# Ten side chains of a hybrid decoder step issued later or on VectorE, and a residual added over two down groups

## The chip, the cores and the metric

The kernel runs on one core of a Trainium2 chip, as one launch. The time is the device time of that core in microseconds (us). The engines are named as in the profile: PE (matmul), PEld (weight load), DVE (VectorE), ACT (ScalarE), POOL (GpSimd) and SP (SyncE, which issues most DMAs).

## The reference

One decoder layer for 1024 prompt positions and 64 sample positions (8 sequences of 8 new tokens), which share the weights:

```python
x = x + 0.5 * swiglu(rmsnorm(x), ffn1_w_gu, ffn1_w_down)        # FFN1, D_MODEL 1024, D_FF 2816
h = rmsnorm(x); z = h @ w_in
y_att = attend(q, k, v, rel_bias)      # 3 head groups (window, dilation) (128,1) (512,4) (2048,16), combined by softmax denominators
xc = causal_conv(xr); hr = rglru(xc)   # recurrent branch, 768 wide
y_rec = gelu(yr) * hr
y_mem = memory_attention(qm, mk, mv)   # 4 heads, 256 memory tokens
merged = sum_b sigmoid(gate_b) * (y_b @ W_b_o);  x = x + merged @ w_out
x = x + 0.5 * swiglu(rmsnorm(x), ffn2_w_gu, ffn2_w_down)        # FFN2
y = rmsnorm(x, final_norm)
```

The sample positions attend to cached keys and values of up to 2048 positions, as well as to each other.

## The kernel before

All data is float32. Every large product is made of three matmuls on split operands (`mac3`, lines 262, 263 and 264: high times high, high times low, low times high), so each weight tile has to be split first: ACT copies the high part (L167), DVE subtracts it for the low part (L168).

The order on PE, ACT, DVE and POOL is that in which the Python code issues the instructions. Only SP's order is left to the scheduler. Each engine takes its instructions in order, so an instruction that waits holds up all that stand behind it.

**Ticks.** `mac3` calls `tick()` in the middle of a long product, and the tile routines call it at the end of one. A tick runs what `later(n, f)` has put n ticks ahead, then, every second tick, one step (up to the next `yield`) of each of the first two generators in `K.side`; odd ticks serve `K.first`. So a further `yield` means that the rest of a side chain is issued two ticks later, behind more matmuls. `drain(*K.side)` at the end of a stage calls `tick()` with no product between, until the side chains are through.

**FFN start** (`operands_of_blocks`, `norms_of_blocks`, `gain_blocks`, `sums_of_blocks`): squares on ACT (L411) are added up on DVE (L413), then `rstd` reduces them with small matmuls (L294) and `put_rows` spreads the result with transposes (L306, L307). Meanwhile PE runs the first `plain` products; their results stay in PSUM banks (`held`) until the row is known, and `evacuate(n)` says how many may stay. `sums_of_blocks` subtracts blocks (L437) that the later operands `put(tp, 6)` and `put(tp, 7)` need.

**FFN middle**: the `quad` loop forms gate and up products, `swiglu` evacuates them on DVE (L539, L554, L561), and `gated_hidden` issues silu, product and store 4, 5 and 7 ticks later (1, 3 and 4 for the last `ALONE` units). `first_hidden` loads back the first four hidden tiles and splits them (`hidden`, L573 on ACT, L574 on DVE). `down` then goes over groups of hidden rows, and each result tile is added to x (L648). In FFN2 `residual(o)` loads a row of the old x (`xr`) and adds it on POOL eight ticks later (L1822); it is called for all eight rows of x in group 1.

**FFN1 end**: for each row tile, `sumsq` squares on ACT and adds on POOL (L321), or on DVE into `odd`; `norm_chunk` then makes the row as above.

**Attention and sample chain**: the heads loop runs on PE with `heads_prep` at the side. `sample_job` is another side chain. For each of three groups, `sample_scores` goes over 16 steps: fetch a key piece and a broadcast query `qb` (DMA from `qs_d`, SP), multiply on POOL (L978, 128x1024), and one step later sum on DVE (L968). Then, for each group and half q, `sample_values` makes the softmax (L1004 to L1012), pads the transposed weights (L1020 to L1025), multiplies by the cached values (L1041, L1043, added up by L1047 or L1049) and selects the heads (L1051, L1053). At the end `sample_mix` combines the groups and transposes (L1068).

**LRU stage**: six `lru_tile`s, each with two z tiles of `w_in` and some gate tiles, a convolution on DVE (L1312 to L1321), gate products (L1332), scan on DVE (L1360) and gelu. `att_combine` is a side chain there: it transposes finished rows (L835), and `mix_groups` weights and adds up the three groups (L858 to L876). The rest of `sample_job` runs at the side too. PSUM banks with the tag "t" are two, shared by L835, the sample chain and others. The stage ends with

```python
            while K.due:
                K.tick()
            drain(*K.side)
```

In the order that the code issues, `sample_job` ends at tick 928 and the last product of the stage is at tick 930. The merge follows.

Of the kernel before, what the change touches and what calls it, by code (L numbers as in the profile page):

```python
# [12 lines left out]
OP = mybir.AluOpType  # L13
# [9 lines left out]
KF = DFF // 128  # L23
# [22 lines left out]
PLAIN, ALONE = 3, 2  # L46
# [14 lines left out]
class Kernel:  # L61
# [329 lines left out]
    def norms_of_blocks(self, tp, xs, pool, eng):  # L391

        nc = self.nc

        def rstd(j, acc):
            r = self.rstd(TC, acc)
            t0 = tp * TH + j * TC

            def put_rows():
                self.rows(self.rbc[:, t0:t0 + TC], r, TC)  # L400
                self.known.add((tp, j))
            self.later(3, put_rows)
        for j in range(2):
            acc = pool.tile([128, TC], F32, name=self.uid("acc"), tag="mu", bufs=2)
            for i in range(2):
                for k in range(4):
                    if i or k:
                        t = self.sums.tile([128, 512], F32, name=self.uid("sq"), tag="s2", bufs=2)[:, :TC]
                    else:
                        t = acc  # L410
                    nc.scalar.activation(t, self.block(xs, i, j)[:, k], AF.Square)  # L411
                    if i or k:
                        eng.tensor_tensor(out=acc, in0=acc, in1=t, op=OP.add)  # L413
                if i:
                    self.later(3, lambda j=j, acc=acc: rstd(j, acc))
                yield

    def gain_blocks(self, xs, g, eng):
# [13 lines left out]
    def sums_of_blocks(self, tp, xs, eng, rest=lambda: True):  # L432

        b11, b12, b21, b22 = (self.block(xs, i, j) for i in range(2) for j in range(2))

        def less(out, x, y):
            eng.tensor_tensor(out=out, in0=x, in1=y, op=OP.subtract)  # L437
        less(b11, b12, b11)
        less(b12, b22, b12)
        less(b22, b22, b11)  # L440
        yield
        yield
        self.put(tp, 6, b22)
        yield
        self.put(tp, 7, b12)
        less(b21, b21, b22)
        yield
        while not rest():
            yield
        self.put(tp, 5, b11)  # L450
        yield
        self.put(tp, 4, b21)
        yield

    def plain(self, gu, p, order, pool):

        nc = self.nc
        ws = [self.unit(gu, 128) for _ in range(2)]
        for tp in order:
            xo = self.xo[tp]  # L460
            sl, uu = (pool.tile([128, 2, TC], F32, name=self.uid(x), tag=x, bufs=n) for x, n in (("sl", 3), ("uu", 3)))
            for j, ms in enumerate(((1, 2), (0, 3))):
                rb = self.rbc[:, tp * TH + j * TC:tp * TH + (j + 1) * TC]
                both = []
                self.evacuate(1)
                for w in ws:
                    while not all(m in xo for m in ms):
                        self.tick()
                    ps = self.mm_bank("pg")
                    self.mac3(ps[:, :TC], [(w(k, 0), (xo[ms[k // 4]][:, 0, k % 4, :], xo[ms[k // 4]][:, 1, k % 4, :]))  # L470
                                           for k in range(KD)])
                    both.append(ps)

                def evac(j=j, rb=rb, both=both, sl=sl, uu=uu, tp=tp):
                    for t, ps in zip((sl, uu), both):
                        nc.vector.tensor_tensor(out=t[:, j], in0=ps[:, :TC], in1=rb, op=OP.mult)
                    if j:
                        self.gated_hidden(p, tp, sl, uu, (2, 3, 4))
                self.held.append(((tp, j), evac))
                self.evacuate(2)  # L480
                if self.first:
                    self.tick()
        for _ in ws:
            self.done()
# [44 lines left out]
    def swiglu(self, p, tp, pool):  # L529

        nc = self.nc
        rb = self.rbc[:, tp * TH:(tp + 1) * TH].rearrange("p (j n) -> p j n", j=2)
        t = {}

        def new(name, shape, bufs):
            t[name] = pool.tile([128, *shape], F32, name=self.uid(name), tag=name, bufs=bufs)

        def plus(out, ps, x):
            nc.vector.tensor_tensor(out=out, in0=ps, in1=x, op=OP.add)  # L539

        def step(m, ps):
            if m == 1:
                new("mu", [TC], 2)
                nc.scalar.activation(t["mu"], ps, AF.Copy)
            if m == 6:
                plus(t["mu"], ps, t["mu"])
            if m == 7:
                new("uu", [2, TC], 3)
                plus(t["uu"][:, 1], ps, t["mu"])
            if m == 5:  # L550
                plus(t["uu"][:, 1], ps, t["uu"][:, 1])
            if m == 2:
                new("sl", [2, TC], 3)
                nc.vector.tensor_tensor(out=t["sl"][:, 0], in0=ps, in1=rb[:, 0], op=OP.mult)  # L554
            if m == 4:
                plus(t["uu"][:, 0], ps, t["mu"])
                nc.gpsimd.tensor_tensor(out=t["uu"], in0=t["uu"], in1=rb, op=OP.mult)
            if m == 3:
                sl = t["sl"]
                plus(sl[:, 1], ps, t["mu"])  # L560
                (nc.gpsimd if p < KF - ALONE else nc.vector).tensor_tensor(out=sl[:, 1], in0=sl[:, 1], in1=rb[:, 1], op=OP.mult)  # L561
                self.gated_hidden(p, tp, sl, t["uu"], (4, 5, 7) if p < KF - ALONE else (1, 3, 4))
        return step

    def hidden(self, k, pool, raws, wait):
# [15 lines left out]
    def first_hidden(self, pool, raws, rest):  # L581

        self.h = {}
        for k in range(2):
            self.hidden(k, pool, raws, 4 + 2 * k)
        for k in range(2, 4):
            self.later(3 + 2 * k, lambda k=k: self.hidden(k, pool, raws, 4))
        self.later(2, rest)

    def gate_up(self, gu, first, pool, copies, misc, change):  # L590
# [23 lines left out]
    def down(self, dn, pool, raws, after, residual=None):  # L614

        for g, (k, nk, w) in enumerate(DOWN):
            ks = range(k, k + nk)
            if 0 < g < len(DOWN) - 1:
                for j in range(2):
                    self.hidden(DOWN[g + 1][0] + j, pool, raws, 8 + 4 * j)  # L620
            if w == D:
                units = [self.unit(dn, w) for _ in ks]
                for c in range(3):
                    for o in range(KD):
                        self.down_tile([u(0, o * 128) for u in units], ks, o, c)
                        after(c, o)
                for _ in ks:
                    self.done()
                continue
            for o0 in range(0, KD, w // 128):  # L630
                wd = self.unit(dn, w)
                for o in range(o0, o0 + w // 128):
                    for c in range(3):
                        self.down_tile([wd(j, (o - o0) * 128) for j in range(nk)], ks, o, c, residual and g == 0)
                    if residual and g == 1:
                        residual(o)
                self.done()

# [213 lines left out]
    def mix_groups(self, o, A, H):  # L852

        nc = self.nc
        m = lambda g: o[:, g, :, H * 64:H * 64 + H]
        l = lambda g: o[:, g, :, H * 65:H * 65 + H]
        w = self.small.tile([128, 5, A, H], F32, name=self.uid("mw"), tag="mw", bufs=2)
# [6 lines left out]
        for g in range(3):  # L864
            t = w[:, 3] if g == 0 else w[:, 4]
# [5 lines left out]
            nc.vector.tensor_tensor(out=w[:, g], in0=w[:, g], in1=w[:, 4], op=OP.mult)  # L871
        oa = [o[:, g, :, 0:H * 64].rearrange("p a (h e) -> p a h e", h=H) for g in range(3)]
        for g in range(3):
            nc.gpsimd.tensor_tensor(out=oa[g], in0=oa[g], in1=w[:, g, :, :, None].to_broadcast([128, A, H, 64]), op=OP.mult)
            if g:
                nc.gpsimd.tensor_tensor(out=oa[0], in0=oa[0], in1=oa[g], op=OP.add)  # L876


    def sample_open(self, pool):
# [67 lines left out]
    def sample_scores(self, g):  # L947

        nc, p = self.nc, self.sp
# [18 lines left out]
            nc.vector.tensor_reduce(st[:, b, :, u * 4:(u + 1) * 4].rearrange("p h t -> p t h"),  # L968
                                    qb.rearrange("p t (h e) -> p t h e", h=4), axis=AX.X, op=OP.add)
        cur = fetch(0)  # L970
        yield
        prev = None
        for n in range(16):
            if n:
# [9 lines left out]
    def sample_values(self, st, g, v_new, qz, k_new):  # L984
# [17 lines left out]
        for q in range(2):  # L1002
# [11 lines left out]
            pad = p.tile([128, 4, 8, 32], F32, name=self.uid("pad"), tag="qb", bufs=2)  # L1014
            if g:
                nc.gpsimd.memset(pad[:, :, :ncl, :], 0.0)
            yield
            yield
            pp = self.bank("t")
# [277 lines left out]
    def lru_tile(self, i):  # L1297
# [5 lines left out]
        fin = p.tile([128, 36], F32, name=self.uid("fin"), tag="fin", bufs=1)  # L1303
        smp = lambda ap: ap[:, SEQ + 3:SEQ + 91].rearrange("p (b u) -> p b u", u=11)
        samp = lambda ap: ap.rearrange("p (b t) -> p b t", b=8)
        nc.gpsimd.memset(xe[:, 0:3], 0.0)
        nc.gpsimd.tensor_copy(smp(xe)[:, :, 0:3], samp(self.stT[:, i, 0:24]))

        def conv(c, ps):
            t0, n = CH[c]  # L1310
# [254 lines left out]
def emit(K):  # L1565
# [98 lines left out]
    with ExitStack() as es:  # L1664
# [6 lines left out]
        def part(c, o):  # L1671
# [3 lines left out]
                K.new_xg(c)  # L1675
                acc[c] = K.tmps.tile([128, CMAX], F32, name=K.uid("acc"), tag="acc", bufs=2)[:, :n]
            K.split_x(c, o, xa, K.v["mix_norm"])
            if c == 2 and o % 2:
                K.sumsq(o // 2, xa, odd, n, nc.vector)
            else:  # L1680
                K.sumsq(o, xa, acc[c], n)
            if o % 4 == 3:
                nc.sync.dma_start(K.x_d[0][:, o - 3:o + 1, t0:t0 + n], K.x[:, o - 3:o + 1, t0:t0 + n])
            if o == KD - 1:
                K.later(6 if c < 2 else 2, lambda: K.norm_chunk(c, 5 if c < 2 else 2, acc[c], *([odd] if c == 2 else [])))
        K.down("w_dn1", pool, K.raw_tiles(pool), after)
        K.tick()
    low.close()
# [270 lines left out]
```

## Time and profile before

| | |
|---|---|
| time, median of 3 runs | 2748.76 us (2747.99 to 2752.01) |
| the profiled execution | 2746.11 us |
| its span | 2744.3 us |
| mean granted TensorE clock | 0.989 |

The profile is of one execution. The busy share of PE is that of matmuls with modelled ends. "Idle before, releaser" in a row is the time for which the engine stood still just before the instruction, and what ended it. PEclk is the clock that was granted, as a share of 2.4 GHz: 1.00 or 0.50 (1.2 GHz).

### The profile page before, as it was taken

How to read it: one execution, taken by the hardware profiler on the slowest of the kernel's cores; microseconds unless marked ns; L12 is line 12 of the kernel's file. 1: busy time of each engine (PE TensorE's matmuls, PEld its weight loads, DVE VectorE, ACT ScalarE, POOL GpSimd, SP SyncE). 2: the span in 40 equal slices, each digit the busy share in tenths (PEclk: the TensorE clock that was granted, in tenths of full speed). 3: DMA queues.
4: the chain of work that ended last, by engine and by line, in shares of the span. 5: the costliest groups of instructions: out<-in, count | busy, mean ns of one | idle time of the engine just before them, and what ended most of it. 6: DMA issues, size and time to landing. Idle time of an engine off the chain costs nothing.

```text
span 2744.3 us, 46291 instructions
## 1 busy us (share of the span) xinstructions
PE 2658.8 (97%) x18088; PEld 2578.8 (94%) x18088; DVE 1728.8 (63%) x3032; ACT 910.3 (33%) x1747; POOL 834.4 (30%) x751
## 2 busy tenths in 40 slices
PE   7999999999999999999989999999999999999997
PEld 7999999899999899989978889999999999999997
DVE  7766566777774433546577755863766666576776
ACT  6332323311153312323334543422542232242112
POOL 2365555200030000324353411231225555553003
PEclk9999999999999999999999999999999999999998
DMA  4222323522243342655544442754424455445221
GB/s 150 70 94 84 103 99 108 206 96 92 76 166 126 96 148 75 208 181 159 174 156 136 138 134 94 262 178 164 149 98 176 163 186 189 168 157 173 96 73 66
DMA packets 181403, 374.98 MB, mean 137 GB/s; under 512 B 21768, under 2 KB 116168, under 8 KB 180416
## 3 DMA queue, kind: packets, MB, share of 16 engines
q1 hardware_dynamic: 166464, 303.85, 33.7%
q0 software_dynamic: 2048, 43.65, 4.7%
q10 hardware_dynamic: 12672, 24.52, 2.4%
q8 instruction: 142, 2.33, 0.4%
q14 instruction: 77, 0.63, 0.1%
HBM read 305.59 MB, written 113.16 MB: 153 GB/s over the span
## 4 chain that ended last, share of the span: by engine, by line
PE 83%; DVE 10%; ACT 2%; issue 2%; DMA 2%; POOL 1%; SPq 0%; DVEq 0%; ACTq 0%; POOLq 0%
PE pg L262 9%; PE pg L264 9%; PE pg L263 9%; PE z L262 7%; PE z L263 7%; PE z L264 7%; PE pd L262 6%; PE pd L263 6%; PE pd L264 6%; DVE ws L168 2%; PE po L264 2%; PE po L263 2%; PE po L262 2%; PE o L814 1%; PE wo L262 1%
## 5 line engine op out<-in xcount | busy, mean ns | idle before, releaser
L262 PE MATMUL pg<-xo,ws 128*128 128x272 f32 x2512 | 730.3, 291 | 18.6 <-DVE uu L539 10.6
L264 PE MATMUL pg<-xo,ws 128*128 128x272 f32 x2512 | 727.0, 289 | 5.2 <-DVE ws L168 5.2
L263 PE MATMUL pg<-xo,ws 128*128 128x272 f32 x2512 | 726.7, 289 | 0.0
L167 ACT ACTIVATE ws<-wr 128x512 fp32r<-128x512 f32 (+1 forms) x550 | 324.9, 613 | 839.9 <-PE pd L264 363.9
L168 DVE TENSOR_TENSOR ws<-wr,ws 128x512 fp32r<-128x512 f32 (+1 forms) x550 | 439.4, 822 | 133.7 <-ACT ws L167 133.3
L262 PEld LDWEIGHTS pg<-xo,ws 128*128 128x128 f32 x2512 | 476.5, 190 | 21.3 <-DVE uu L539 12.8
L264 PEld LDWEIGHTS pg<-xo,ws 128*128 128x128 f32 x2512 | 476.4, 190 | 5.8 <-DVE ws L168 5.8
L262 PE MATMUL z<-xg,ws 128*128 128x368 f32 (+1 forms) x1392 | 478.9, 344 | 0.0
L263 PEld LDWEIGHTS pg<-xo,ws 128*128 128x128 f32 x2512 | 476.8, 190 | 0.0
L264 PE MATMUL z<-xg,ws 128*128 128x368 f32 (+1 forms) x1392 | 460.2, 331 | 0.0
L263 PE MATMUL z<-xg,ws 128*128 128x368 f32 (+1 forms) x1392 | 459.8, 330 | 0.0
L262 PE MATMUL pd<-h,ws 128*128 128x368 f32 (+1 forms) x1056 | 348.7, 330 | 3.7 <-DVE x L648 2.6
L263 PE MATMUL pd<-h,ws 128*128 128x368 f32 (+1 forms) x1056 | 346.8, 328 | 0.0
L264 PE MATMUL pd<-h,ws 128*128 128x368 f32 (+1 forms) x1056 | 345.9, 328 | 0.0
L648 DVE TENSOR_TENSOR x<-x,pd 128x368 f32<-128x368 f32 (+1 forms) x504 | 258.0, 530 | 137.6 <-PE pd L264 133.8
L262 PEld LDWEIGHTS z<-xg,ws 128*128 128x128 f32 x1392 | 265.2, 191 | 15.7 <-issue 14.2
L263 PEld LDWEIGHTS z<-xg,ws 128*128 128x128 f32 x1392 | 265.5, 191 | 1.4 <-issue 0.2
L264 PEld LDWEIGHTS z<-xg,ws 128*128 128x128 f32 x1392 | 264.1, 190 | 0.0
L262 PEld LDWEIGHTS pd<-h,ws 128*128 128x128 f32 x1056 | 199.3, 189 | 4.3 <-DVE x L648 2.9
L264 PEld LDWEIGHTS pd<-h,ws 128*128 128x128 f32 x1056 | 199.4, 189 | 0.0
L263 PEld LDWEIGHTS pd<-h,ws 128*128 128x128 f32 x1056 | 199.4, 189 | 0.0
L978 POOL TENSOR_TENSOR qb<-qb,kv 128x1024 f32<-128x1024 f32 x48 | 116.2, 2424 | 198.0 <-DMA qb<-qs_d 146.6
(297 smaller groups left out, 3705.0 us busy)
## 6 DMA issues: line engine op xcount, KB each, us to landing
wr<-in_w_gu_dram SPq DMA_DIRECT2D x96, 512.0 KB
wr<-in_w_in_dram SPq DMA_DIRECT2D x58, 512.0 KB
qb<-qs_d SPq DMA_DIRECT2D x48, 512.0 KB
h_d<-sl ACTq DMA_DIRECT2D x88, 272.0 KB
hr<-h_d SPq DMA_DIRECT2D x44, 544.0 KB
wr<-in_w_dn_dram SPq DMA_DIRECT2D x44, 512.0 KB
out_sk_dram<-in_cache_k_dram POOLq DMA_DIRECT2D x16, 1020.0 KB, 6.9
out_sv_dram<-in_cache_v_dram POOLq DMA_DIRECT2D x16, 1020.0 KB, 8.3
```

The source lines that it names most:

```text
L167: nc.scalar.activation(spl[:, 0, :n], src, AF.Copy)
L168: nc.vector.tensor_tensor(out=spl[:, 1, :n], in0=src, in1=spl[:, 0, :n].bitcast(F32), op=OP.subtract)
L262: nc.tensor.matmul(out, wh, xh, start=start and i == 0, stop=False, **more)
L263: nc.tensor.matmul(out, wh, xl, start=False, stop=False, **more)
L264: nc.tensor.matmul(out, wl, xh, start=False, stop=i == n - 1, **more)
L648: nc.vector.tensor_tensor(out=xa, in0=xa, in1=ps[:, :n], op=OP.add)
L814: nc.tensor.matmul(po[:, e], pt[:, h, j * 128:(j + 1) * 128], z["vt"][:, kb[j], e], start=j == 0, stop=j == len(kb) - 1)
L978: nc.gpsimd.tensor_tensor(out=prev, in0=prev, in1=kk, op=OP.mult)
```

## The change

It shifts when side work is issued, at ten places:

1. FFN start: `rstd` five ticks after the squares instead of three, `put_rows` four instead of three; `evacuate` lets one more held product stay.
2. `sums_of_blocks`: the three subtractions are issued over three steps instead of one, and all that follows is a step later.
3. `ALONE` units: silu, product, store after 1, 2 and 5 ticks instead of 1, 3 and 4.
4. `first_hidden`: hidden tiles 0 and 1 are split one tick later; tiles 2 and 3 are loaded one tick earlier and split one tick later.
5. FFN1 end: the sum of row tile 6 of the last chunk goes to DVE, its `rstd` is a tick later; the rows of the first two chunks are made a tick later.
6. `sample_scores`: three `yield`s instead of one after the first fetch.
7. `sample_values`: three `yield`s instead of two before the transposes.
8. `lru_tile`: the zero fill and the copy into `xe` on DVE.
9. `mix_groups`: its five large operations on DVE.
10. FFN2: the residual is added for even rows in group 1 and for odd rows in group 2 of `down`.

```diff
@@ norms_of_blocks
-            self.later(3, put_rows)
+            self.later(4, put_rows)
...
-                    self.later(3, lambda j=j, acc=acc: rstd(j, acc))
+                    self.later(5, lambda j=j, acc=acc: rstd(j, acc))
@@ sums_of_blocks
         less(b11, b12, b11)
+        yield
         less(b12, b22, b12)
+        yield
         less(b22, b22, b11)
-        yield
         yield
@@ plain
-                self.evacuate(1)
+                self.evacuate(2)
...
-                self.evacuate(2)
+                self.evacuate(3)
@@ swiglu
-                self.gated_hidden(p, tp, sl, t["uu"], (4, 5, 7) if p < KF - ALONE else (1, 3, 4))
+                self.gated_hidden(p, tp, sl, t["uu"], (4, 5, 7) if p < KF - ALONE else (1, 2, 5))
@@ first_hidden
-            self.hidden(k, pool, raws, 4 + 2 * k)
+            self.hidden(k, pool, raws, 5 + 2 * k)
...
-            self.later(3 + 2 * k, lambda k=k: self.hidden(k, pool, raws, 4))
+            self.later(2 + 2 * k, lambda k=k: self.hidden(k, pool, raws, 6))
@@ down
-                    if residual and g == 1:
+                    if residual and g == 1 + o % 2:
@@ mix_groups
-            nc.gpsimd.tensor_tensor(out=oa[g], in0=oa[g], in1=w[:, g, :, :, None].to_broadcast([128, A, H, 64]), op=OP.mult)
+            nc.vector.tensor_tensor(out=oa[g], in0=oa[g], in1=w[:, g, :, :, None].to_broadcast([128, A, H, 64]), op=OP.mult)
...
-                nc.gpsimd.tensor_tensor(out=oa[0], in0=oa[0], in1=oa[g], op=OP.add)
+                nc.vector.tensor_tensor(out=oa[0], in0=oa[0], in1=oa[g], op=OP.add)
@@ sample_scores
         cur = fetch(0)
-        yield
+        for _ in range(3):
+            yield
@@ sample_values
                 nc.gpsimd.memset(pad[:, :, :ncl, :], 0.0)
+            yield
             yield
             yield
@@ lru_tile
-        nc.gpsimd.memset(xe[:, 0:3], 0.0)
-        nc.gpsimd.tensor_copy(smp(xe)[:, :, 0:3], samp(self.stT[:, i, 0:24]))
+        nc.vector.memset(xe[:, 0:3], 0.0)
+        nc.vector.tensor_copy(smp(xe)[:, :, 0:3], samp(self.stT[:, i, 0:24]))
@@ the end of FFN1
-            if c == 2 and o % 2:
+            if c == 2 and (o % 2 or o == 6):
...
-                K.later(6 if c < 2 else 2, lambda: K.norm_chunk(c, 5 if c < 2 else 2, acc[c], *([odd] if c == 2 else [])))
+                K.later(6 if c < 2 else 3, lambda: K.norm_chunk(c, 6 if c < 2 else 2, acc[c], *([odd] if c == 2 else [])))
```

## Rows read from the trace of the kernel before

**Rows 1.** The page of the profile, part 1: busy time of each engine, its share of the span, and instructions.

```profile
PE 2658.8 (97%) x18088; PEld 2578.8 (94%) x18088; DVE 1728.8 (63%) x3032; ACT 910.3 (33%) x1747; POOL 834.4 (30%) x751
```

**Rows 2.** The waits of PE: what waited, for what; total us, times, the longest in us.

```profile
PE pg L262 <- DVE uu L539: 10.6, 10, 3.1
PE t L1020 <- ACT ss L1012: 8.3, 1, 8.3
...
PE t L294 <- DVE acc L413: 7.1, 2, 6.8
...
PE s L785 <- DVE s L788: 5.4, 1, 5.4
PE pg L264 <- DVE ws L168: 5.2, 2, 2.6
PE t L294 <- POOL acc L321: 5.1, 2, 2.9
PE g L1332 <- DVE xc L1321: 3.5, 1, 3.5
PE t L835 <- DVE ss L1009: 3.5, 1, 3.5
PE t L835 <- DVE sel L1047: 2.9, 2, 2.0
PE pd L262 <- DVE x L648: 2.6, 1, 2.6
```

**Rows 3.** Busy time of each engine in four stretches: from and to, length, busy us (instructions) of PE, PEld, DVE, ACT and POOL, granted clock, DMA share, GB/s.

```profile
41.20:48.00 6.80, 5.05 (x23) 5.02 (x24) 5.89 (x15) 4.40 (x12) 1.57 (x2) 0.50 0.00 0
...
1198.30:1205.10 6.80, 5.90 (x22) 5.01 (x22) 4.64 (x9) 2.24 (x9) 1.74 (x1) 0.50 0.71 244
1389.40:1396.20 6.80, 5.73 (x15) 4.74 (x16) 6.59 (x12) 3.32 (x5) 0.20 (x1) 0.50 0.53 175
1430.40:1437.20 6.80, 3.42 (x12) 3.39 (x13) 4.70 (x9) 4.00 (x8) 3.45 (x8) 0.50 0.18 59
```

**Rows 4.** The FFN start: the timelines of DVE and POOL (start, us, engine, line, operation, output and inputs, count, idle before), all instructions of line 413 (duration in ns: shortest, median, longest), and the busy times of the stretch behind it (columns as in rows 3).

```profile
33.83 10.55 DVE L413 TENSOR_TENSOR acc<-acc,sq 128x272 f32<-128x272 f32 x8
...
34.03 8.57 POOL L425 TENSOR_TENSOR xs<-xs,vec 128x1088 f32<-128x1088 f32 x4
...
L413 DVE TENSOR_TENSOR acc<-acc,sq x56: 420/442/2055, 16.8 to 1992.7; 128x272 f32<-128x272 f32 x56
...
46.00:89.00 43.00, 40.41 (x316) 40.15 (x316) 35.32 (x50) 21.29 (x36) 11.05 (x9) 0.98 0.22 69
```

**Rows 5.** The timeline of DVE at the second stall of the FFN1 start.

```profile
80.66 1.29 DVE L437 TENSOR_TENSOR xs<-xs 128x1088 f32<-128x1088 f32 x1
```

**Rows 6.** The timeline of DVE around the step from gate and up products to the down products of FFN1.

```profile
511.15 1.29 DVE L574 SCALAR_TENSOR_TENSOR h<-hr,h 128x1088 fp32r<-128x1088 f32 x1 [2.57 <-ACT h L573]
...
521.92 1.41 DVE L648 TENSOR_TENSOR x<-x,pd 128x352 f32<-128x352 f32 x3
```

**Rows 7.** The sample scores beside the heads: the timelines of POOL and DVE.

```profile
1184.48 2.40 POOL L978 TENSOR_TENSOR qb<-qb,kv 128x1024 f32<-128x1024 f32 x1 [5.64 <-DMA qb<-qs_d]
1192.69 2.36 POOL L978 TENSOR_TENSOR qb<-qb,kv 128x1024 f32<-128x1024 f32 x1 [5.81 <-DMA qb<-qs_d]
...
1195.08 1.22 DVE L968 TENSOR_REDUCE sst<-qb 128x16 f32<-128x1024 f32 x1 [6.02 <-POOL qb L978]
```

**Rows 8.** The first tiles of the LRU stage: timelines of POOL and DVE, all instructions of line 874 (duration in ns, shortest, median and longest), and the busy times of the stretch.

```profile
1383.17 2.88 POOL L978 TENSOR_TENSOR qb<-qb,kv 128x1024 f32<-128x1024 f32 x1 [2.32 <-DMA qb<-qs_d]
...
1386.12 0.46 DVE L1318 TENSOR_SCALAR xc<-xe,vec 128x352 f32<-128x352 f32 x1 [1.90 <-POOL xe L1306]
...
1428.94 2.51 DVE L1360 TENSOR_TENSOR_SCAN lB<-lA,lS 128x1112 f32<-128x1112 f32 x1
...
L874 POOL TENSOR_TENSOR oc<-oc,mw x24: 606/613/1712, 1425.4 to 1565.6; 128x256 f32<-128x256 f32 x24
...
1386.00:1450.00 64.00, 52.15 (x280) 48.24 (x279) 55.16 (x94) 27.92 (x38) 33.37 (x36) 0.89 0.44 136
```

**Rows 9.** The residual of FFN2: the timeline of POOL.

```profile
2518.96 2.87 POOL L1822 TENSOR_TENSOR x<-x,xr 128x1088 f32<-128x1088 f32 x1 [0.66 <-DMA xr<-x_d]
```

**Rows 10.** The last steps of the sample chain at the end of the LRU stage: the timelines of PE, DVE, ACT and POOL.

```profile
1657.34 0.27 PE L1004 MATMUL t<-ident,sst 128*128 128x128 f32 x1
...
1661.40 0.28 DVE L1008 TENSOR_TENSOR ss<-t,sbc 128x128 f32<-128x128 f32 x1
...
1662.65 0.19 ACT L1012 ACTIVATION_READ_ACCUMULATOR ss<-ss,ogl 128x1 f32 x1
...
1669.15 0.29 DVE L1025 COPY pad<-t 128x128 f32<-128x128 f32 x1 [1.47 <-ACT ptn L1023]
...
1680.44 0.36 ACT L1049 ACTIVATE sel<-t 128x256 f32<-128x256 f32 x1
...
1686.01 0.61 DVE L1053 TENSOR_REDUCE ogl<-sel 128x64 f32<-128x256 f32 x1
...
1693.96 0.23 DVE L866 TENSOR_TENSOR mw<-mw,ogl 128x2 f32<-128x2 f32 x2
...
1698.78 0.46 POOL L876 TENSOR_TENSOR ogl<-ogl 128x128 f32<-128x128 f32 x1
...
1699.29 0.66 PE L1068 MATMUL t<-ident,ogl 128*64 128x128 f32 x8
```

## The prediction

> **What bounds the kernel now.** I read the page's first part, then the waits of PE, then the clock by stretch, then the timelines around each wait. PE is busy for 2658.8 of 2744.3 us [rows 1], and the change adds and removes no matmul. So the time can only move by what PE waits, and by the stretches in which its clock is down. The waits [rows 2] name the ten places where PE stands longest for a side chain; together they hold 54 us. The second loss is the clock: four of the stretches behind such waits are 6.8 us long at a granted clock of 0.50 (1.2 GHz) [rows 3]. In each the work would take half the time at 1.00, so the loss is half of PE's busy time there: 2.5 us at 41, 3.0 at 1198, 2.9 at 1389, 1.7 at 1430. A wait that goes takes its clock loss with it.
>
> A tick is one product, and a side step comes every second one. At the end of the LRU stage nine steps lie between L1004 at 1657.3 and L1068 at 1699.3 [rows 10]: 4.7 us a step. This is what a further `yield` gives a chain, as long as products are left to give it.
>
> **Edit 1, FFN start.** The wait of 6.8 us [rows 2] is for DVE's sum, and with 2.5 us of clock it costs 9.3. DVE was not idle: its eight adds took 10.55 us, 1.3 each against a median of 0.44, beside four POOL products of 2.1 each [rows 4]. Issuing `rstd` two products later lets PE do work first that it now does afterwards, and DVE's work is all still there. What is gained is limited by what DVE has free afterwards, 43.0 - 35.3 = 7.7 us [rows 4]. Between 0 and 7.7 I take 4.
>
> **Edit 2, sums.** PE waits 2 x 2.6 us for L168 [rows 2] because DVE has subtractions (L437, 1.29 us each) in front of it [rows 5]. Spreading them over three steps leaves the total of DVE's work ahead of that split as it is. Bounds 0 and 5.2; near the lower one, 0.5.
>
> **Edits 3 and 4, hidden tiles.** The waits for L539 are 10.6 us in ten pieces over both FFNs, the longest 3.1 [rows 2]. That one is the split L574, which DVE reached early and for which it stood 2.57 us, with `uu` behind it [rows 6]. Splitting a tick later takes that away. But shortly after, the down products need banks that L648 frees, and L648 started only at 521.92 [rows 6], behind the last gate product's chain. Edit 3 issues silu and product earlier, but its store a tick later, so what PE gains before it is mostly given back there. Bounds -3 (the store one or two products late) and +10.6; I take 1.5.
>
> **Edit 5, FFN1 end.** PE waits 5.1 us in two pieces for POOL's L321, the longest 2.9 [rows 2]; that one is the one here. One of POOL's adds goes to DVE, and the row is made a product later. Bounds 0 and 5; 2.5.
>
> **Edit 6, scores.** The wait of 5.4 us at L785, with 3.0 of clock, costs 8.4 [rows 2, 3]. DVE reached L968 of the scores 6.02 us before POOL had its product ready; POOL in turn waited 5.81 for the DMA of `qb`, and two products started 8.2 us apart [rows 7], where a step would be 4.7 if it is as long here. So the chain falls behind with each step, and its L968 holds up the softmax of the heads, which stands behind it in DVE's order. Two more steps in front give it some 9 us of start, more than the 6.02. The rate stays, so it may fall behind again. Bounds 0 and 8.4; 6.
>
> **Edits 7, 8 and 9, LRU stage.** Four waits: 3.5 (L1332), 8.3 (L1020), 3.5 and 2.9 (L835), 18.2 together [rows 2], and 2.9 + 1.7 of clock [rows 3], so 22.8. One by one. At L1332, DVE stood 1.90 us for POOL's copy into `xe`, which stood behind a score product of 2.88 [rows 8]; on DVE that goes, and I let the clock's 2.9 go with it: 4.8. At L1020, DVE ran the scan of 2.51 us ahead of the softmax [rows 8]; a further step gives 4.7 of the 8.3: 5. The waits at L835 are for a bank that late DVE readers hold; the chains shift against each other, so any of them may go or come: 4 of 6.4. Sum 14, bounds 0 and 22.8. What edit 9 costs: DVE takes five operations for each of nine mixes. POOL's took 0.61 at the median [rows 8]; DVE's nearest rows are 0.28 for 128x128 and 0.61 for a reduction of 128x256 [rows 10], so 1.4 to 3.0 a mix. DVE is busy for 55.2 of the first 64 us [rows 8], and its 8.8 free us hide two mixes; if they weren't free the price would be 3 a mix.
>
> One row bears on all that moves between POOL and DVE. L413 takes up to 2055 ns against a median of 442 while POOL's products of 2.1 us run [rows 4]: one add is held for about one POOL instruction. The Trainium skill, "SBUF — State Buffer", section "Who interferes with whom", says why: VectorE instructions with two SBUF inputs and GpSimd ones that read SBUF take a shared port under an exclusive lock for the whole instruction, and the other blocks. The trace agrees, 2.06 against 2.1. By that rule edits 8 and 9 relieve DVE, and edit 6 burdens it; the latter is the third rival below.
>
> **Edit 10, residual.** The wait of 2.6 us for L648 [rows 2] is beside POOL's adds of 2.87 us, whose `xr` came late [rows 9]. With every second row in another group, half as many fall together: 2.6, bounds 0 and 2.6.
>
> **What the further steps cost at the end.** `sample_job` now ends at tick 928 and the last product of the stage is at tick 930. Edit 6 adds two steps for each of three groups, edit 7 one for each of six halves: 12 steps, 24 ticks, so the end would be at tick 952. About eleven steps are then run by `drain` with no product between, and PE's own small matmuls of the chain wait, one behind the other, with the merge behind them. From the rows of before [rows 10], PE would wait: for the softmax, from L1008 at 1661.40 to the end of L1012 at 1662.84, 1.4; for the copies into `pad` and their hop, about 0.6; then, after the value products, 0.36 (L1049), about 1.1 (L1051 and L1053, 0.61), about 0.9 for the mix's first half with its exponential, 1.3 for the second (1693.96 to POOL's start near 1695.3), and the five operations, which POOL finished at 1699.24, 3.9, and for which DVE would take 1.4 or so: 5.1. With hops some 8 us, and a fall of the clock of 2.5 to 3.0 [rows 3]: 11. Bounds 6 (no fall of the clock and shorter hops) and 16.
>
> **Sum.** 4 + 0.5 + 1.5 + 2.5 + 6 + 14 + 2.6 = 31.1 gained, 11 lost: 20 less. On the profiled execution's 2746.11 us (span 2744.3) that is 2726; the median of the runs is 2.65 above that execution, so **2729 us**.
>
> **The rivals.**
>
> *All the waits go* (0.17). If the shifted chains meet no new collisions, the LRU stage gives 22.8, the scores 8.4, the FFN start 7.7 and the rest 7: 46, less 8 at the end: 38 less, 2711. For it: none of these waits is at a place where DVE is full for the whole stage (63% over the span [rows 1]). Against it: DVE is at 86% in the first LRU tiles [rows 8], and in the FFN starts it never stood still.
>
> *The waits only move* (0.14). PE meets the next reader that is late: LRU 4, scores 3, the others 9, and 16 at the end: no change that can be told, about 2749. For it speaks that L835's waits are collisions of two chains and not the length of one. Against it, that two waits (L1332, L539) have a cause that the edits take away.
>
> *Slower by the late scores* (0.12). Edit 6 ends the scores six steps later, inside the LRU tiles, where L978 still runs at 1383 [rows 8]. Each step brings DVE its L968 of 1.22 us [rows 7] and, by the adds [rows 4], up to 1.6 us of being held: 6 x 2.8 = 17 us, of which 8.8 are free [rows 8]: 8 us more of waits. If the chain stays late beside that, scores and LRU give nothing: 11.1 gained, 11 + 8 lost, 2757. It decides from the point where PE waits in the LRU tiles over 25 us as it does now and the drain costs its 11.
>
> **Chances and range.** The forecast has 0.57, its own range 2716 to 2743. About 0.2% (5.5 us) is what can be told from no change. Faster 0.74, same 0.14, slower 0.12. The range, 2706 to 2752, takes in the first two rivals and leaves out most of the third.
>
> **What the profile after would show.** Right: no wait of 5 us at L785, none of over 5 at L1020, no `xe` from POOL, and at the end of the LRU stage new waits of PE of about 1.4, 0.6 and 5, at L1020, L1041 and L1068, with a clock of 0.50 behind. The FFN1 start keeps a wait for L413, shorter than 6.8. Wrong: if the end of the stage shows no such waits, the count of steps has failed; if L835 and L1332 stay, or L168 takes their place, the LRU term; if the time gained at L539 comes back as a wait for L648, only the small term of edits 3 and 4 is touched. The sum falls most easily with LRU's 14 and the drain's 11, both of which hang on where chains meet.

## The result, and the profile after

The changed kernel takes 2788.54 us (median of 4 runs, 2785.81 to 2790.19) against 2748.38 before (4 runs): a ratio of 1.0142, 95% interval 1.0125 to 1.016. It is slower by 40 us where I forecast 20 less. The span of the profiled execution is 2787.3 us, 43.0 more than before. Part 1 of its page, beside [rows 1]:

```profile
PE 2673.7 (96%) x18088; PEld 2591.0 (93%) x18088; DVE 1751.5 (63%) x3090; ACT 912.3 (33%) x1747; POOL 804.1 (29%) x693
```

The matmuls are the same, yet PE is busy for 14.9 us more: that much is the lower clock (mean 0.979 for 0.989). The other 28 us are waits. The waits of PE, beside [rows 2] (total us, times, longest):

```profile
PE t L306 <- POOL rs L299: 13.0, 4, 9.3
PE pg L262 <- ACT ws L167: 10.8, 2, 8.4
PE g L1335 <- ACT lA L1336: 10.7, 2, 6.2
PE pg L262 <- ACT sq L411: 9.0, 1, 9.0
...
PE o L815 <- ACT pt L805: 6.4, 6, 2.0
PE g L1335 <- issue: 6.0, 1, 6.0
PE t L1071 <- DVE ogl L877: 5.2, 1, 5.2
PE pd L262 <- DVE sl L540: 5.2, 1, 5.2
PE s L786 <- DVE s L789: 4.1, 1, 4.1
```

Lines behind 439 are one to three higher than before, in the experiments none to three, by the edits that are in (before, L1335 was L1332, L306 is the same). The old long waits at L1020 (8.3), L294 (6.8) and L1332 (3.5) are gone as such. New ones stand at or shortly behind nearly every place that was edited.

PE's order at the products (L262) did not change, so I compare the start of the same product, for instance the first `mk` product (823.8 us before, 838.3 after). What the delay grows by from one such product to the next is the stage's loss, in us of the profiled execution. "Forecast" is the sum of the prediction, split by stage; the split of edits 1 to 4 between the two FFNs was made for this table.

| stage (edits) | forecast | measured |
|---|---|---|
| FFN1 start (1, 2) | -4.2 | +4.1 |
| FFN1 turn to down products (3, 4) | -1.0 | +2.4 |
| FFN1 end (5) | -2.5 | +7.6 |
| heads (6) | -6 | +10.0 |
| LRU tiles (6, 7, 8, 9) | -14 | +4.6 |
| drain (6, 7) | +11 | +14.9 |
| FFN2 start and turn (1 to 4) | -0.8 | +1.6 |
| residual (10) | -2.6 | -2.6 |

The rest of the 43.0 is 0.4 in stages without edits. Six of the seven stages with a forecast gain lose.

**FFN1 start.** The first product after the row has a bank of PSUM to wait for. Timelines of PE and DVE:

```profile
39.46 0.57 PE L262 MATMUL pg<-xo,ws 128*128 128x272 f32 x1 [9.00 <-ACT sq L411]
50.94 0.57 PE L262 MATMUL pg<-xo,ws 128*128 128x272 f32 x1 [2.78 <-DVE rs L298]
...
28.49 6.86 DVE L379 SCALAR_TENSOR_TENSOR xo<-xs,vec,xo 128x272 fp32r<-128x272 f32 x8
...
39.18 0.14 DVE L298 TENSOR_SCALAR rs<-t 16x1 f32<-16x1 f32 x1
```

PE starts 0.14 us after DVE has read `rstd`'s bank (39.32). The profile names ACT here, whose squares PE doesn't need; for the next such wait, of 2.78 us, it names L298, with the same distance of some 0.15. The code gives this stage eight banks. What `evacuate` counts as one held product is a pair, gate and up, in two banks; PE has done six products by then, so three held pairs take six. The second `rstd` and the row's transposes (L306, copied out from 39.24 on) take the others. DVE reads the second `rstd` late: L379 takes 6.86 us, and the adds stand behind it. That it is the banks is read from these rows, not tested by itself.

**FFN1 end.** DVE, ACT and PE:

```profile
805.16 0.49 DVE L1093 SCALAR_TENSOR_TENSOR mg<-mraw,vec,mg 128x256 fp32r<-128x256 f32 x1 [9.20 <-ACT mg L1092]
...
806.87 0.15 DVE L298 TENSOR_SCALAR rs<-t 112x1 f32<-112x1 f32 x1
...
804.62 0.51 ACT L1092 ACTIVATE mg<-mraw,vec 128x256 fp32r<-128x256 f32 x1 [7.98 <-DMA mraw<-in_mem_dram]
...
808.67 0.90 PE L306 MATMUL t<-ident,rs 128*128 128x128 f32 x3 [9.29 <-POOL rs L299]
```

One tick later, the row's small DVE operations stand behind `mem_prep` (L1093), a side chain that waits for the load of the memory tokens. DVE is idle for 9.20 us with the row in its queue. Before, the row was ahead of the same wait, which cost PE nothing:

```profile
790.14 0.15 DVE L298 TENSOR_SCALAR rs<-t 112x1 f32<-112x1 f32 x1
799.33 0.48 DVE L1090 SCALAR_TENSOR_TENSOR mg<-mraw,vec,mg 128x256 fp32r<-128x256 f32 x1 [9.04 <-ACT mg L1089]
```

**Heads.** SP's timeline, then POOL's and DVE's:

```profile
1229.82 0.49 SPq L911 DMA_DIRECT2D qs_d<-stok  x1
1230.36 3.46 SPq L915 DMA_DIRECT2D out_sk_dram<-stok  x8
1233.93 2.64 SPq L915 DMA_DIRECT2D out_sv_dram<-sv  x8
1236.66 0.39 SPq L964 DMA_DIRECT2D qb<-qs_d  x1
...
1241.63 2.34 POOL L980 TENSOR_TENSOR qb<-qb,kv 128x1024 f32<-128x1024 f32 x1 [12.26 <-issue]
...
1244.01 1.22 DVE L969 TENSOR_REDUCE sst<-qb 128x16 f32<-128x1024 f32 x1 [8.88 <-POOL qb L980]
```

Two steps later, the last fetch of the first group stands in SP's queue behind seventeen stores of the next group's preparation. DVE, which stands 8.88 us for this product, has the heads' softmax behind it: PE waits 4.1 us at L786 and 6.4 in six pieces at L815, where before it waited 5.4 at L785 alone. Before, the fetch was ahead of the stores:

```profile
1198.11 0.39 SPq L963 DMA_DIRECT2D qb<-qs_d  x1
...
1206.18 0.49 SPq L910 DMA_DIRECT2D qs_d<-stok  x1
```

**LRU tiles.** DVE and ACT around the waits at L1335, and the busy times of a stretch (columns as in [rows 3]):

```profile
1439.46 2.25 DVE L869 TENSOR_TENSOR mw<-mw 128x4 f32<-128x4 f32 x1
...
1448.25 2.24 DVE L1360 COPY lS<-stT 128x8 f32<-128x8 f32 x1
...
1470.21 6.15 DVE L1324 SCALAR_TENSOR_TENSOR xc<-xe,vec,xc 128x368 f32<-128x368 f32 x3
...
1424.71 0.21 ACT L863 ACTIVATE mw<-mw 128x12 f32<-128x12 f32 x1 [8.07 <-DVE mw L862]
...
1459.40:1484.00 24.60, 11.78 (x49) 9.57 (x48) 23.93 (x41) 3.01 (x6) 9.48 (x7) 0.78 0.56 175
```

Score products (L980) now run to 1484.6, beside the convolution. An operation of 128x4 (L869) takes 2.25 us where it mostly takes 0.16, a copy of 128x8 (L1360) 2.24, and L1324 6.15 for three where 1.8 is usual. ACT stands 8.07 us for the mix's weights, with the gates' sigmoid (L1336) behind it. In the last stretch shown DVE is busy for 23.93 of 24.60 us.

**Drain.** PE, and its clock over 13.7 us (columns as in [rows 3]):

```profile
1736.58 0.47 PE L1023 MATMUL t<-ident,ss 128*128 128x128 f32 x1 [2.06 <-ACT ss L1014]
1738.01 1.08 PE L1044 MATMUL t<-kv,pad 128*32 128x256 f32 x8 [0.75 <-DVE pad L1028]
1745.28 1.12 PE L1071 MATMUL t<-ident,ogl 128*64 128x128 f32 x8 [5.17 <-DVE ogl L877]
...
1735.80:1749.50 13.70, 7.00 (x37) 4.55 (x38) 6.13 (x28) 2.24 (x7) 0.00 (x0) 0.50 0.09 22
```

Three waits, 8.0 together (forecast 1.4, 0.6 and 5.1, with hops 8), and half of 7.0 as clock.

### The profile page after: what moved, and what is told of

It reads as the page before. It is cut to its first block, busy times and chain, and to the rows that moved or that the text cites. A ratio compares the mean times of both kernels' runs of the same rounds, so it can differ in the third digit from the quotient of the medians.

```text
span 2787.3 us, 46285 instructions
## 1 busy us (share of the span) xinstructions
PE 2673.7 (96%) x18088; PEld 2591.0 (93%) x18088; DVE 1751.5 (63%) x3090; ACT 912.3 (33%) x1747; POOL 804.1 (29%) x693
## 4 chain that ended last, share of the span: by engine, by line
PE 80%; DVE 12%; issue 3%; ACT 3%; DMA 2%; POOL 1%; SPq 0%; DVEq 0%; ACTq 0%; POOLq 0%
PE pg L262 9%; PE pg L264 9%; PE pg L263 9%; PE z L262 7%; PE z L263 6%; PE z L264 6%; PE pd L262 6%; PE pd L263 6%; PE pd L264 6%; DVE ws L168 2%; PE po L264 2%; PE po L263 2%; PE po L262 2%; PE wo L262 1%; PE wo L263 1%
## 5 line engine op out<-in xcount | busy, mean ns | idle before, releaser
L262 PE MATMUL pg<-xo,ws 128*128 128x272 f32 x2512 | 729.8, 291 | 30.9 <-ACT ws L167 10.8
L168 DVE TENSOR_TENSOR ws<-wr,ws 128x512 fp32r<-128x512 f32 (+1 forms) x550 | 447.2, 836 | 162.0 <-ACT ws L167 161.7
L262 PEld LDWEIGHTS pg<-xo,ws 128*128 128x128 f32 x2512 | 476.2, 190 | 33.9 <-ACT ws L167 11.0
L262 PE MATMUL z<-xg,ws 128*128 128x368 f32 (+1 forms) x1392 | 484.9, 348 | 2.1 <-DVE ta L1396 2.1
L262 PE MATMUL pd<-h,ws 128*128 128x368 f32 (+1 forms) x1056 | 348.5, 330 | 6.8 <-DVE sl L540 5.2
L262 PEld LDWEIGHTS z<-xg,ws 128*128 128x128 f32 x1392 | 267.5, 192 | 19.1 <-issue 14.3
L262 PEld LDWEIGHTS pd<-h,ws 128*128 128x128 f32 x1056 | 199.0, 188 | 7.8 <-DVE sl L540 5.5
L980 POOL TENSOR_TENSOR qb<-qb,kv 128x1024 f32<-128x1024 f32 x48 | 117.4, 2449 | 220.2 <-DMA qb<-qs_d 136.2
```

The source lines that it names most:

```text
L168: nc.vector.tensor_tensor(out=spl[:, 1, :n], in0=src, in1=spl[:, 0, :n].bitcast(F32), op=OP.subtract)
L262: nc.tensor.matmul(out, wh, xh, start=start and i == 0, stop=False, **more)
L980: nc.gpsimd.tensor_tensor(out=prev, in0=prev, in1=kk, op=OP.mult)
```

## The experiments

The theory: each loss is an order, something put behind an instruction that waits. The rival: DVE is full wherever the kernel loses. The stages are apart in time, so one kernel puts one question to each. Of "no steps" to "first group early" there is one run each, so a stage is judged by all the kernels that share an edit. The diffs are against the changed kernel; "undone" means the line of the kernel before.

**Without the chain's steps.** Edits 6 and 7 undone, and:

```diff
-                self.evacuate(2)
+                self.evacuate(1)
...
-                self.gated_hidden(p, tp, sl, t["uu"], (4, 5, 7) if p < KF - ALONE else (1, 2, 5))
+                self.gated_hidden(p, tp, sl, t["uu"], (4, 5, 7) if p < KF - ALONE else (1, 3, 4))
...
-                K.later(6 if c < 2 else 3, lambda: K.norm_chunk(...))
+                K.later(6 if c < 2 else 2, lambda: K.norm_chunk(...))
```

> The changed kernel without edits 6 and 7 (the sample chain has its old number of steps), and at three earlier places with one half of an edit undone: evacuate holds as few products as before (rstd stays later), ALONE steps are (1, 3, 4) again, and the last row of FFN1 is made after 2 ticks again. The stages follow each other on PE, so each is read by itself, against the kernel before. Theory: the longer sample chain costs the heads their 9.9 us and the drain its 14.9, so both come out within 1 of the kernel before; the LRU stage with edits 8 and 9 alone comes out 3 to 8 us faster than before. FFN1 start: the held banks cost it, so 0 to -3 in place of +4.1. FFN1 turn: 0 to -2 in place of +2.4 if the later store of edit 3 costs it. FFN1 end: -1 to -3 in place of +7.6, since the row's small DVE operations stand in front of those that wait for the memory tokens' DMA. Rival, that DVE is full wherever it loses: FFN1 start stays near +4, and the LRU stage stays at +3 to +5, because edits 8 and 9 put more on DVE.

**Scores later only.** Edits 4 and 7, the later `rstd` and `put_rows`, and `o == 6` on DVE undone:

```diff
-            yield
             yield
             yield
             pp = self.bank("t")
...
-            self.later(4, put_rows)
+            self.later(3, put_rows)
...
-                    self.later(5, lambda j=j, acc=acc: rstd(j, acc))
+                    self.later(3, lambda j=j, acc=acc: rstd(j, acc))
```

> The changed kernel without edit 7 (edit 6 kept: scores two steps later per group), with rstd and put_rows as early as before (evacuate holds one more), edit 4 undone (edit 3 kept), and row tile 6 of FFN1 summed on POOL again (the later tick kept). Theory: heads +9 to +11 as in the changed kernel, since edit 6 alone acts there; LRU +3 to +8; five or six steps are left to the drain, so it costs 6 to 9 in place of 14.9. FFN1 start +3 to +5 by the held banks; FFN1 turn +1 to +3 by edit 3; FFN1 end +6 to +9 by the later tick. Rival: the heads lose by something else than edit 6 (the order of the queue that loads), so they come out below +5; FFN1 end loses by the sum moved to DVE, so it comes out below +2 here.

**Values later only.** Edits 1, 3, 4, 5 and 6 undone:

```diff
-        for _ in range(3):
-            yield
+        yield
```

> The changed kernel without edit 6 (edit 7 kept: values one step later per half), and without edits 1, 3, 4 and 5. Theory: heads 0; LRU stage faster than before by 3 to 10, as the scores end where they did; six steps in the drain, so 6 to 9 as in the run before this one. FFN1 start: only edit 2 is left, -1 to +1. FFN1 turn and FFN1 end: 0. Rival, that the values and not the scores disturb the LRU tiles: LRU stays at +3 or more here and is near 0 with the scores alone.

**Copy on DVE only.** Edits 1, 2, 6, 7 and 9 undone, and of edit 5 all but the rows of the first two chunks:

```diff
-            nc.vector.tensor_tensor(out=oa[g], in0=oa[g], in1=w[:, g, :, :, None].to_broadcast([128, A, H, 64]), op=OP.mult)
+            nc.gpsimd.tensor_tensor(out=oa[g], in0=oa[g], in1=w[:, g, :, :, None].to_broadcast([128, A, H, 64]), op=OP.mult)
```

> The changed kernel without edits 6, 7 and 9 (edit 8 kept: the copy into xe on DVE), without edits 1 and 2, and of edit 5 only the later rows of the first two chunks. Edits 3 and 4 are kept. Theory: heads and drain 0; LRU -2 to -5 by edit 8 alone, so that edit 9 is the difference to the run without the chain's steps; FFN1 start 0 within 0.5; FFN1 turn +2.4 as in the changed kernel; FFN1 end 0 to -1. Rival: edit 8 gives nothing, because DVE takes over the same wait.

The losses by stage against the kernel before, as above, with the later runs beside (FFN1 turn and down in one row; small stages left out):

| stage | after | no steps | scores | values | copy | no hidden shift | products | first group early | four parts | with sums |
|---|---|---|---|---|---|---|---|---|---|---|
| FFN1 start | +4.1 | -1.4 | -5.8 | +4.7 | +0.1 | +3.9 | +3.1 | -0.3 | -5.0 | -6.0 |
| FFN1 turn, down | +2.9 | +2.5 | +0.6 | +0.6 | +3.2 | +0.8 | +2.0 | +2.9 | -0.1 | +0.2 |
| FFN1 end | +7.6 | +1.4 | +8.4 | 0.0 | -0.7 | +7.2 | +7.9 | +7.5 | +0.6 | -0.7 |
| heads | +10.0 | -4.2 | +1.4 | -0.6 | -2.6 | +12.1 | +9.7 | -3.3 | -0.6 | -3.9 |
| LRU tiles | +4.6 | -4.4 | +13.7 | -3.1 | -6.6 | +4.0 | +5.1 | +9.6 | -9.1 | -6.9 |
| drain | +14.9 | -0.2 | +8.6 | +7.9 | -0.2 | +15.2 | +8.7 | +11.1 | -0.2 | -0.2 |
| merge | 0.0 | 0.0 | +0.1 | 0.0 | 0.0 | +0.1 | +8.3 | +0.1 | 0.0 | 0.0 |
| FFN2 start | +1.1 | +3.1 | +1.4 | +1.4 | +0.2 | +1.0 | +1.0 | +1.1 | +0.2 | +2.6 |
| residual | -2.6 | -2.8 | -2.7 | -2.8 | -2.8 | -2.8 | -2.8 | -2.8 | -2.8 | -2.8 |

These four took 2742.28, 2773.18, 2755.17 and 2737.31 us, one run each beside 2745.51 of before. *FFN1 end*: +7.2 to +8.4 in all five kernels with the later tick, at most +1.4 without it. That +1.4 is the one kernel with the sum on DVE and without the tick, where PE waits 3.5 us for DVE's L321; with the tick the sum on DVE costs nothing that can be seen (7.2 to 7.9 against 8.4). The wait of the scores run, which has the sum on POOL:

```profile
PE t L306 <- POOL rs L299: 9.9, 1, 9.9
```

*Drain*: 8.6 and 7.9 with six steps, 14.9 with twelve, 0 with none. *LRU tiles*: -3.1 to -9.1 with the scores as early as before, +4.0 to +13.7 with them late. The later values gain nothing there. *FFN1 start*: the expectation that the held banks alone cost it missed. Holding one more product with `rstd` early gains 5.8; with both the gain is gone (-0.3 to +4.1 in four kernels). *FFN1 turn*: the store of edit 3 is not the cause (0.6 with edit 3 alone); it goes with edit 4 (2.0 to 3.2 in the five kernels that have it, -0.1 to 0.8 in the others). The heads gave +1.4 with edit 6, neither of the numbers expected.

The rival fails where the run without steps decides it: with edits 8 and 9 in, the LRU tiles gain 4.4 there where the rival says a loss of 3 to 5, and the FFN1 start gains 1.4 where it says a loss of about 4. In the LRU tiles of the changed kernel the rival is right in part: with the late scores DVE is full in the stretch shown. Missed besides: the heads of the run without steps (-4.2 for 0), the LRU tiles of the scores run (+13.7 for +3 to +8) and the FFN1 start of the values run (+4.7 for -1 to +1).

**No hidden shift.** Of the changed kernel, only edit 4 undone:

```diff
-            self.hidden(k, pool, raws, 5 + 2 * k)
+            self.hidden(k, pool, raws, 4 + 2 * k)
...
-            self.later(2 + 2 * k, lambda k=k: self.hidden(k, pool, raws, 6))
+            self.later(3 + 2 * k, lambda k=k: self.hidden(k, pool, raws, 4))
```

> The changed kernel with edit 4 alone undone (first_hidden splits and loads as before). In the runs so far the turn from gate and up to down products of FFN1 lost 2.0 to 2.7 us wherever edit 4 was in and 0.1 to 0.6 where it was not, and the order of SP's DMAs, which the scheduler plans over the whole kernel, differed from that of the kernel before among the heads in the two runs with edit 4 although nothing was edited there; their heads came out 2.6 and 4.2 us faster, those of the run without it 0.6. Theory: edit 4 costs the turn 2.4, so +0 to +0.6 here; and it is the order of SP that makes the heads cost 9.9 in the changed kernel, so that with edit 4 undone they cost 0 to 5 though edit 6 is still in. Rival: the heads lose by edit 6 itself, +9 to +11 here too. LRU and drain: +3 to +14 and 14 to 15, as the twelve steps are in.

2787.31 us. The turn falls from +2.4 to +0.4, so edit 4 costs 2. PE's waits from 505 to 530 us, in the changed kernel and here:

```profile
PE pd L262 <- DVE sl L540: 5.2, 1, 5.2
PE pg L262 <- DVE uu L540: 1.3, 1, 1.3
```

```profile
PE pg L262 <- DVE uu L540: 4.8, 2, 4.1
PE pd L262 <- DVE x L649: 0.4, 1, 0.4
```

The wait for `uu` (4.1) that edit 4 takes away comes back as one of 5.2 at the first down products. For the heads my theory fell: +12.1, so edit 4's effect on SP's order isn't what they lose by.

**Products for the end.**

```diff
-FILL = (5, 5, (1, 1, 1, 2, 2, 2))
+FILL = (5, 5, (1, 1, 1, 2, 2, 4))
```

> The whole changed kernel, with the two gate tiles that are left for the start of the merge run at the end of the LRU stage (the last number of FILL 4 in place of 2). They are six products, 12 ticks, so six of the eleven steps at the end get matmuls beside them. Theory (the drain is steps without products): up to the first product of the merge the loss against the changed kernel falls by 5 to 8 us; what is left in the drain is one wait of about 5 before the last transposes and a stretch of clock at 0.50, and the waits of 2.06 and 0.75 are gone. All before stays within 1. Rival: the chain's own length at the end bounds it, or the start of the merge misses the tiles that covered its loads: no gain, within 2 of the changed kernel.

2789.61 us. The drain falls by 6.2 as expected, and the merge loses 8.3. PE at the seam, the step from the LRU stage to the merge:

```profile
1763.21 1.12 PE L1071 MATMUL t<-ident,ogl 128*64 128x128 f32 x8 [5.16 <-DVE ogl L877]
1766.27 0.67 PE L263 MATMUL po<-ys,ws 128*128 128x368 f32 x1 [1.33 <-DVE ys L1444]
1773.72 0.43 PE L262 MATMUL po<-ys,ws 128*128 128x368 f32 x1 [2.11 <-ACT ys L1443]
```

The waits of 1.33 and 2.11 are for the splits of the merge's operands (L1444, L1443), which the two tiles had covered; what else the 8.3 holds is not told apart. So steps without products are what the drain costs, and these products can't be spared elsewhere.

**Four parts**, and **with sums**: the kernel before with these parts of the change; the second has edit 2 too.

```diff
-                self.evacuate(1)
+                self.evacuate(2)
...
-                self.evacuate(2)
+                self.evacuate(3)
...
-                    if residual and g == 1:
+                    if residual and g == 1 + o % 2:
...
-        nc.gpsimd.memset(xe[:, 0:3], 0.0)
-        nc.gpsimd.tensor_copy(smp(xe)[:, :, 0:3], samp(self.stT[:, i, 0:24]))
+        nc.vector.memset(xe[:, 0:3], 0.0)
+        nc.vector.tensor_copy(smp(xe)[:, :, 0:3], samp(self.stT[:, i, 0:24]))
...
-                K.later(6 if c < 2 else 2, lambda: K.norm_chunk(c, 5 if c < 2 else 2, ...))
+                K.later(6 if c < 2 else 2, lambda: K.norm_chunk(c, 6 if c < 2 else 2, ...))
```

> The kernel before with four parts of the change alone: evacuate holds one more product (edit 1 without the later rstd), the rows of the first two chunks of FFN1 a tick later (part of edit 5), the copy into xe on DVE (edit 8), the residual over two groups (edit 10). Theory, by the stages measured so far: FFN1 start -6 to -10, FFN1 end -0.5, heads -1 to 0 if SP's order stays, LRU -5 to -7, residual -2.7: 14 to 20 us less than before. Rival: holding one more product only helps beside edit 2 (both were in the run that gained 5.8 at the start), so the start gives 0 and the sum is 8 to 11; or SP's order changes the heads by up to 4 either way.

> The run with four parts, and edit 2 (the subtractions spread over three steps) beside. Edit 2 alone cost the FFN1 start 4.7 and the FFN2 start 1.4. Theory: it costs 3 to 5 in the FFN1 start and 1.4 in the FFN2 start here too, so 4 to 6 slower than the run without it; the FFN1 start is -5.8 as in the run that had both. Rival: beside the held product it costs nothing, both starts are alike in the two runs.

2727.71 and 2728.98 us (4 runs each) against 2750.11 of before (7 runs): ratios 0.9921 (0.9906 to 0.9936) and 0.9925 (0.9909 to 0.9942). Both beat both kernels. By the medians that is 22.4 and 21.1 us less than before; the profiled spans, which the stages add up to, are 16.6 and 17.1 shorter. In the first of the two, the longest wait left in the FFN1 start behind the first load (L294), those of the LRU tiles, and ACT in the LRU tiles:

```profile
PE g L1332 <- ACT lA L1333: 7.3, 2, 6.1
PE t L294 <- DVE rbc L307: 6.4, 1, 6.4
...
PE t L835 <- ACT sel L1049: 2.4, 1, 2.4
PE t L1020 <- ACT ss L1012: 2.0, 1, 2.0
...
1397.47 0.21 ACT L862 ACTIVATE mw<-mw 128x12 f32<-128x12 f32 x1 [9.95 <-DVE mw L861]
```

The held product does help alone: -5.0. Edit 2 costs nothing beside it in FFN1 (-6.0), where alone it cost 4.7 in one kernel; in the FFN2 start it costs 2.4. The two medians are 1.3 apart, not the 4 to 6 expected.

**First group early.** The whole change, but:

```diff
-        for _ in range(3):
+        for _ in range(1 if g == 2 else 3):
             yield
```

> The whole changed kernel, but the scores of the first group (the one with window 2048, which runs beside the heads) start after one step as before; the other two groups wait three. In the changed kernel SP issues the fetch of the last qb of the first group at 1236.66, behind 17 stores of the next group's preparation that it had from 1229.82 on, and POOL stands 12.26 us before the product at 1241.63; in the kernel before the last fetch is issued at 1198, ahead of those stores. Theory: two steps later put the last fetches of the first group behind the stores, and this is what the heads cost; so they come out at -4 to +3 here, in place of +9.9, as in the runs without edit 6. The LRU stage has scores four steps later and not six: +1 to +8; the drain runs nine or ten steps: 13 to 15. Rival: the heads lose by edit 6 in any group, or by where the changed kernel stands against its DMAs, and stay at +7 to +12.

2773.36 us. The heads come out at -3.3 and not +10: their loss was the first group's place in SP's queue. Its timeline:

```profile
1211.58 0.39 SPq L964 DMA_DIRECT2D qb<-qs_d  x1
1218.88 0.33 SPq L938 DMA_DIRECT2D kv<-in_cache_k_dram  x1
1219.31 0.49 SPq L911 DMA_DIRECT2D qs_d<-stok  x1
```

The last fetch is ahead of the stores again. The LRU tiles (+9.6) and the drain (+11.1) came out beside the +1 to +8 and 13 to 15 expected. That the scores run lost only 1.4 with edit 6 fits in direction alone: there one fetch more was ahead of the stores (issued at 1209.62, stores from 1212.48), but what put it there is not settled.

## Why the prediction was wrong

The forecast was 20 us less, and 40 more came. The step that failed is the same in most terms of the sum: each moved chain is credited with what it gains at its head, and what it is put behind, on every queue that it uses, stands at nothing. Only the drain has a price for it. By stage, the LRU tiles came out 19 us worse than forecast, the heads 16, the end of FFN1 10 and its start 8.

**Right.** The drain was counted and sized: waits of 8.0 for 8, in the order named. Its 14.9 for 11 is, as far as the rows tell, the chain's own matmuls, which have moved behind the last product, and the clock. The residual came within 0.2 of its 2.6 in all ten kernels. The third rival, the late scores in the LRU tiles, is what the stage did. I gave it 0.12 and 2757, and counted nothing beside it.

**Edit 1.** The step that failed is "lets PE do work first that it now does afterwards". It takes a free bank to do so. I counted DVE's time and not the banks: eight, of which the held pairs take six while an `rstd` and a row wait to be read. Holding one more is worth 5 to 6 without the later `rstd` (three kernels), and nothing or a loss beside it. I also wrote that DVE never stood still in the FFN starts; [rows 4] have it idle for 7.7 of 43.0 us. Of edit 2, "leaves the total as it is" is not borne out either: alone 4.7 more (one kernel), beside the held product nothing.

**Edits 3 and 4.** "Mostly given back" was right as a mechanism, and the size was off: 4.1 for 5.2, so all and a little more. The culprit I named, the store, was wrong, and the bank that the down products wait for comes from the gate products (L540), not from L648.

**Edit 5.** I costed the row "a product later" by the wait that it removes, without asking what DVE is given in that product: `mem_prep`, which waits 8 us for a DMA. The tick cost 7, and the stage lost 7.6 where I forecast 2.5 less.

**Edit 6.** "Two more steps in front give it some 9 us of start" looked at one end of the chain. Its other end moved too, past the stores of the next group on SP's queue, which I had not read through. First group early shows it: 13 of the heads. In the LRU tiles the sum put edit 6 at nothing, and this is the largest miss, a gain of 14 forecast and 4.6 lost: the stage is at -3 or better in the five kernels without edit 6 and at +4 or more in the five with it. The later scores bring DVE their sums and its holds beside L980.

**Edits 7 to 9.** Edit 8 was under-sized: 4.8 forecast, 6.6, 9.1 and 6.9 in the three kernels that have it without edits 6, 7 and 9. But the gain is not only where I put it. In four parts the wait of 3.5 at L1332 for `xc` is gone (the values run, which has edit 8 too, still waits 3.1 for it), and one of 6.1 stands at the same line: ACT waits 9.95 us for the mix's weights (L862), with the gates' sigmoid behind it. What the stage gains on balance are the waits at L1020, from 8.3 to 2.0 without edit 7, and at L835, from 6.4 to 2.4; why they fell is open. Edit 7, 5 forecast, gives nothing that can be seen. Edit 9: DVE takes 0.42 us each (L875, L877), 2.1 a mix, within my bounds; whether it costs PE is not told apart (-4.4 with it, -6.6 to -9.1 without).

**What is open.** Kernels that are alike up to a stage differ there by some us: FFN1 start 4.1, 3.9, 3.1 and -0.3 with the same edits, heads -0.6 to -4.2 in the five without edit 6. SP's order differs among some of the latter, but not between the copy run and four parts (-2.6 and -0.6). A term below some 4 us of one stage is not shown by one kernel, not even its sign; the FFN1 start of the changed kernel is such a one.

## What to carry to other kernels

A step that is issued later is gained at its head and paid for at its tail: list, for each queue it uses (DMA queues too), what it is moved past and what that waits for, count its steps against the products that are left, and count the banks that are held meanwhile. A wait of an in-order engine is priced by all that stands behind it, so the same edit can gain 5 us alone and nothing beside its neighbour. Part a bundle by stage: four of its parts were worth some 20 us (17 by the profiled spans, 22 by the medians) that the others hid.

## What the hardware showed that I had not expected

For its length, a small DVE operation loses most by the hold between DVE and POOL: beside L980, L869 (128x4) took 2.25 us for 0.16, and the copy into `xe` (L1310), 0.172 at the median, up to 2.378. Moving a small operation from POOL to DVE does not always take it out of POOL's way. The Trainium skill, "SBUF — State Buffer", section "Who interferes with whom", names both cases, operations with two SBUF inputs and copies in a 2-port mode; the durations, about one POOL product of 2.4 us each, agree. Whether these copies ran in such a mode no run shows.
